# Attention splits: float16 high parts on ScalarE, remainders on GpSimd, keys and values split directly from PSUM

## The chip, the cores and the metric

The kernel runs on one core of one Trainium2 chip. The metric is the device time of one execution in microseconds. Below, PE is TensorE, DVE is VectorE, ACT is ScalarE, POOL is GpSimd and SP is SyncE, which issues every DMA of this kernel.

## The reference

One transformer-like layer over 1024 latent tokens of width 1024, with 256 context tokens as additional keys. Part of it is latent attention with 8 heads; beside it stand a Fourier mixing branch, gates, one output projection, a residual and a last norm.

```
h      = layer_norm(x) * (1 + scale) + shift            # scale, shift from silu(c)
q_lat, ckv, k_rope, gates, fourier_in = split(h @ w_in + b_in)
q      = rms_norm(q_lat) @ w_q_up                        # 8 heads of 96, rotary on 32
k, v   = rms_norm(ckv) @ w_kv_up                         # keys: context + latents = 1280
attn   = softmax(q @ k^T / sqrt(96)) @ v                 # 8 heads, 1024 queries, 1280 keys
four   = real(fft2(fourier_in)) @ w_fourier + b
y      = concat(attn * silu(g1), four * silu(g2)) @ w_out + b_out
out    = layer_norm(alpha * x + gate * y) * ln_g + ln_b
```

All inputs are float32. To be accurate enough, the kernel writes each matmul operand as a high part and a remainder ("hi" and "lo"), and adds the three leading products.

## The kernel before

Everything up to about 277 us (norms, the input projection, the queries, most of the Fourier branch) and the output projection after about 557 us keep their code. Between them lies attention.

Attention runs over 32 pairs (8 heads, 4 pairs of query tiles each). A pair has two query tiles j = 0, 1 of 128 queries against 1280 keys. For one query tile the steps are:

- `s_lat` (L135 to L137): PE writes the negated scores to the PSUM tile `SS`, three products per block of keys.
- `max_lat` (L1016) on DVE: copies `SS` to the SBUF tile `E` and keeps the row minimum; `bias` (L1023) makes the exponent's bias from it.
- `exp` (L1029) on ACT: `E` becomes the exponentials in float32, with their row sums.
- `hi` (L1040 on POOL, L1038 on ACT): the float16 high part of `E` goes to `EH`. The table `HI_CUTS` says which columns go to which engine: 0 to 639 to POOL ('p'), 640 to 1279 to ACT ('a').
- `lo` (L1046): the remainder `E - hi` in float16, also into `EH`. By `LO_CUTS`, for j = 0 DVE ('v') takes 768 columns and POOL 512; for j = 1 DVE takes 128 and POOL 1152. `HI_LAST` and `LO_LAST` are the same tables for pairs 28 to 31.
- L1050: SP issues a DMA that transposes `EH` into `ET`.
- `pv` (L1063, L1066): PE multiplies `ET` by the split V; `pv_top` (L1072, ACT) and `pv_out` (L1082, DVE) put the result away.

There are three buffers each for `E`, `EH` and `ET` (`EB`, `EHB`, `ETB`). `E` is free for a later tile when its remainder is done, `EH` when its transposing DMA has landed.

A loop over rounds n writes PE's instructions in a fixed order, given by the list `SEQ`: scores of pair n+1, `pv` of pair n-2 (`LAG`), and fills. The order of the other engines' instructions is chosen by the scheduler; each engine then works through its own queue in order. Fills are work for a later head: K^T of a pair of heads (`build_kt`, rounds 4, 5, 12, 13, 20, 21), the second group of V (`build_v(1, ...)`, rounds 14 and 15), the transposed queries (`build_qt`), from round 24 on the preparation of the output projection (`prep`, L1139, L82, L83), whose splits also go through POOL and DVE.

`build_kt` and `build_v` end in `evac`. With pool = "v" (`BP`, `BV`) ACT copies the PSUM tile to an SBUF tile `sp` (L786), POOL takes the high part from it (L787) and DVE the remainder, from `sp` and the high part (L788). With pool = False ACT writes the high part directly from PSUM (L772) and DVE reads PSUM again for the remainder (L774). `build_qt` and the first group of V already use False.

Of the kernel before, what the change touches and what calls it, by code (L numbers as in the profile page):

```python
# [21 lines left out]
P = 128  # L22
D = 1024
T = 1024
# [13 lines left out]
HI_CUTS = eval("(((0, 640, 'p'), (640, 1280, 'a')), ((0, 640, 'p'), (640, 1280, 'a')))")  # L38
LO_CUTS = eval("(((0, 768, 'v'), (768, 1280, 'p')), ((0, 128, 'v'), (128, 1280, 'p')))")
# [6 lines left out]
HI_LAST = eval("(((0, 512, 'p'), (512, 1280, 'a')), ((0, 512, 'p'), (512, 1280, 'a')))")  # L46
LO_LAST = eval("(((0, 512, 'v'), (512, 1280, 'p')), ((0, 320, 'v'), (320, 1280, 'p')))")
LATE = eval('(30, 31, 32, 33)')  # rounds at which further k-tiles of the out projection are prepared
# [6 lines left out]
BP = {"0": False, "1": True, "v": "v"}['v']  # L55
BQ = {"0": False, "1": True, "v": "v"}['0']
BV = {"0": False, "1": True, "v": "v"}['v']
BACC = {'dynamic_dma_scratch_size': int('1024')}  # no DMA is started by GpSimd
LIFT = 15.0 * math.log(2.0)  # the exponentials are scaled by 2**15 to lie well within float16
# [3 lines left out]
def tile_hybrid_block(ctx: ExitStack, tc: tile.TileContext, a, out, dbg=None):  # L63
# [6 lines left out]
    def u4(shape, dt, name):  # L70
        return big.tile(shape, dt, tag="u4", name=name)
# [35 lines left out]
    def rsqrt(y, v, n):  # L107
        """y = (v + EPS) ** -0.5 on a [P, n] tile, refined by one Newton step."""
# [22 lines left out]
    def mm3(ps, pairs, start=True):  # L131
        """ps = sum over (stationary hi, lo, moving hi, lo) of the three leading products."""
        n = len(pairs)
        for i, (sh, sl, mh, ml) in enumerate(pairs):
            nc.tensor.matmul(ps, lhsT=sh, rhs=mh, start=(start and i == 0), stop=False)  # L135
            nc.tensor.matmul(ps, lhsT=sh, rhs=ml, start=False, stop=False)  # L136
            nc.tensor.matmul(ps, lhsT=sl, rhs=mh, start=False, stop=(i == n - 1))  # L137

    # ------------------------------------------------------------ constants
# [9 lines left out]
    # partial rows of the modulation lie at partitions 32j (latents) and 32j+1 (context), two a result  # L149
# [3 lines left out]
    # PSUM pools up to the out projection, and the SBUF pool of the first phases  # L153
# [15 lines left out]
    # ------------------------------------------------------------ loads of the start  # L169
# [8 lines left out]
    class WBlock:  # L178
        """256 columns of w_in, as hi and lo parts, in two halves of k"""
# [23 lines left out]
    class WPack:  # L203
        """three blocks of 256 columns of w_in from one on, their rows in the order in which they are wanted"""
# [24 lines left out]
    mod = const.tile([P, 8, 4], F32, name="mod")  # shift_x, shift_c, 1+scale_x, 1+scale_c  # L229

    w_mod = a["w_ada"].rearrange("(k p) (s c) -> p k s c", p=P, s=3)
    GROUPS = [(i,) for i in range(8)]  # channel tiles whose modulation is worked out together
    ada, ada_ps, ada_rows = {}, {}, {}

    def load_group(g):
        """shift and scale columns of a group's channels"""
# [10 lines left out]
    def ada_mms(g):  # L247
        """partial rows of shift and scale, for the latents and for the context"""
# [11 lines left out]
    def ada_out(g):  # L260
        """their sums, transposed"""
# [44 lines left out]
    # ------------------------------------------------------------ adaLN, h^T and the Fourier input  # L306
    hT = {}  # hi and lo parts by channel tile and half of the tokens
    # the Fourier input and a first block of gates
# [5 lines left out]
    def fm_mms(ps, w, m, half, ks, parts=range(3)):  # L314
        """the leading products of the hi and lo parts, or some of them"""
# [9 lines left out]
    def x_tr(half, dt, ts=range(4)):  # L325
        """a channel tile of the normalised latents, transposed"""
# [27 lines left out]
    def h_first(half, dt):  # L354
        """the same from PSUM, without GpSimd"""
# [16 lines left out]
    def fin_out(half, g):  # L372
        """the Fourier input u as sums and differences of its token halves; the gates"""
# [15 lines left out]
    # gate of the residual branch: partial rows over halves of k, two blocks of 512 columns  # L389
# [20 lines left out]
    def gate_sums():  # L410
        """the gate itself, in the rows 0 and 64"""
# [19 lines left out]
    def warm_up(n):  # L431
        """products of no use that have TensorE's clock up when its work arrives"""
# [88 lines left out]
    # ------------------------------------------------------------ gates  # L521
# [28 lines left out]
    # ------------------------------------------------------------ token-major q | ckv | krope  # L550
# [9 lines left out]
    # tiles 0-7 hold the latents, 8 and 9 the context  # L560
# [11 lines left out]
    def rope(dst, src, cos, sin, n, eng):  # L572
        """dst[P, n, 32] = src * cos + swap_halves(src) * signed sin"""
# [28 lines left out]
    def normalise(t0, t1):  # L602
        """root-mean-square norms of q and ckv (without their weights) and the rotated key"""
# [17 lines left out]
    def latents_t(hf):  # L621
        """q and ckv of four token tiles, transposed"""
# [33 lines left out]
    ckc_k1 = u4([P, 2, 2, TC], F32R, "ckc_k1")  # and the context keys of one set  # L656
# [47 lines left out]
    with tc.manual_schedule(engines={ET.PE}):  # L704
# [11 lines left out]
        # ------------------------------------------------------------ q up-projection, token-major, with rope  # L716
# [4 lines left out]
        def tables(nm, NK):  # L721
            """hi and lo parts of a cosine and a sine table"""
# [23 lines left out]
    # ------------------------------------------------------------ Fourier mixing  # L746
# [7 lines left out]
    def ck(i, hl):  # L754
        """ckv^T of key tile i."""
# [12 lines left out]
    def evac(hi, lo, ps, pool, scale=None):  # L768
        """hi and lo parts of a PSUM tile; lo on VectorE, or from a copy on GpSimd"""
# [37 lines left out]
    def build_v(grp, i2, pool):  # L807
        if grp == 0 and i2 % 2 == 0:
            V[grp, i2 // 2] = u4([P, 2, 2, 4, 2, 64], F16, f"V{grp}{i2}")  # key tile (2), head, hi/lo, channel
# [645 lines left out]
```

## Time and profile before

| what | value |
|---|---|
| time, median of 3 runs | 655.37 us (654.37 to 655.69) |
| profiled execution: span from first to last instruction | 650.7 us |
| PE busy | 591.8 us (91%) |
| DVE busy | 467.6 us (72%) |
| ACT busy | 266.7 us (41%) |
| POOL busy | 334.6 us (51%) |
| DMA queue q1, share of 16 engines | 58.2% |
| mean granted TensorE clock | 0.956 |

The profiled execution has no time of its own beside its span; the median of the timed runs is 4.7 us above that span. Busy shares are means over stages with different limits, so a stage is read from its own stretch. Matmuls overlap in the records, so a PE that is busy all the time may still have some room.

### The profile page before, as it was taken

How to read it: one execution, taken by the hardware profiler on the slowest of the kernel's cores; microseconds unless marked ns; L12 is line 12 of the kernel's file. 1: busy time of each engine (PE TensorE's matmuls, PEld its weight loads, DVE VectorE, ACT ScalarE, POOL GpSimd, SP SyncE). 2: the span in 40 equal slices, each digit the busy share in tenths (PEclk: the TensorE clock that was granted, in tenths of full speed). 3: DMA queues.
4: the chain of work that ended last, by engine and by line, in shares of the span. 5: the costliest groups of instructions: out<-in, count | busy, mean ns of one | idle time of the engine just before them, and what ended most of it. 6: DMA issues, size and time to landing. Idle time of an engine off the chain costs nothing. (4 is left out here: it accounts for less than half of the span.)

```text
span 650.7 us, 9608 instructions
## 1 busy us (share of the span) xinstructions
PE 591.8 (91%) x3491; PEld 474.9 (73%) x3491; DVE 467.6 (72%) x806; ACT 266.7 (41%) x464; POOL 334.6 (51%) x320
## 2 busy tenths in 40 slices
PE   7999999999999999999889978897797879799995
PEld 6887777888899998987657755675475546567884
DVE  5539119501016778789789889989989989899775
ACT  2423421310124444666767765575575543100000
POOL 2023115001013294556979977897699988850000
PEclk8899999999999999999789987899798979999999
DMA  9999136000010322139989997699698998830611
GB/s 282 317 307 346 33 96 238 13 1 0 1 47 3 101 66 66 41 59 166 181 153 187 192 153 134 125 171 176 131 188 171 203 173 184 276 120 23 204 65 64
DMA packets 199703, 88.82 MB, mean 136 GB/s; under 512 B 168204, under 2 KB 189964, under 8 KB 199656
## 3 DMA queue, kind: packets, MB, share of 16 engines
q1 hardware_dynamic: 199656, 88.21, 58.2%
q8 instruction: 27, 0.44, 0.3%
q14 instruction: 20, 0.16, 0.1%
HBM read 41.39 MB, written 4.20 MB: 70 GB/s over the span
## 5 line engine op out<-in xcount | busy, mean ns | idle before, releaser
L1046 POOL TENSOR_TENSOR EH<-E,EH 128x512 f16<-128x512 f32 (+1 forms) x64 | 123.7, 1933 | 2.2 <-ACT EH L1038 0.4
L1029 ACT ACTIVATE E<-E,mx 128x1280 f32<-128x1280 f32 x64 | 87.1, 1362 | 52.3 <-DVE mx L1023 52.0
L1016 DVE TENSOR_SCALAR_CACHE_REDUCE E<-SS 128x1280 f32<-128x1280 f32 x64 | 94.9, 1484 | 12.9 <-PE SS L137 5.4
L1040 POOL TENSOR_SCALAR EH<-E 128x640 f16<-128x640 f32 (+1 forms) x64 | 63.6, 993 | 40.3 <-ACT E L1029 35.8
L1046 DVE TENSOR_TENSOR EH<-E,EH 128x768 f16<-128x768 f32 (+1 forms) x64 | 75.7, 1183 | 6.8 <-POOL EH L1040 6.3
L320 PE MATMUL fin<-h,wh 128*128 128x512 f32 x192 | 65.5, 409 | 0.0
L1063 PE MATMUL pv<-ET,V 128*128 128x256 f16 x320 | 51.3, 296 | 13.8 <-DMA ET<-EH 8.3
L320 PE MATMUL g<-h,wh 128*128 128x512 f32 x192 | 60.3, 394 | 1.0 <-DVE upm L382 1.0
L135 PE MATMUL SS<-KTh,QT 96*128 96x512 f32 x128 | 56.7, 443 | 3.6 <-DVE E L1016 3.0
L1038 ACT ACTIVATE EH<-E 128x640 f16<-128x640 f32 (+1 forms) x64 | 47.8, 747 | 14.2 <-DMA ET<-EH 13.3
L137 PE MATMUL SS<-KTh,QT 96*128 96x512 f32 x128 | 52.3, 408 | 0.0
L136 PE MATMUL SS<-KTl,QT 96*128 96x512 f32 x128 | 52.1, 407 | 0.0
L1063 PEld LDWEIGHTS <-V 128*128 128x128 f16 x320 | 28.9, 104 | 29.7 <-issue 25.3
L351 POOL TENSOR_SCALAR h<-xnT,mod 128x512 f32<-128x512 f32 x15 | 12.8, 853 | 63.6 <-DVE mod L270 30.7
L320 PEld LDWEIGHTS fin<-h,wh 128*128 128x128 f32 x192 | 36.4, 190 | 10.4 <-issue 2.9
L320 PEld LDWEIGHTS g<-h,wh 128*128 128x128 f32 x192 | 36.0, 188 | 9.8 <-issue 1.4
L320 PE MATMUL g<-h,wl 128*128 128x512 f32 x96 | 37.8, 394 | 0.0
L320 PE MATMUL fin<-h,wl 128*128 128x512 f32 x96 | 37.1, 395 | 0.0
L1066 PE MATMUL pv<-ET,V 128*64 128x256 f16 x320 | 36.6, 306 | 0.0
L135 PEld LDWEIGHTS SS<-KTh,QT 96*128 96x128 f32 x128 | 25.2, 197 | 14.1 <-issue 6.5
L1352 POOL TENSOR_TENSOR xr<-xr,lng 128x256 f32<-128x256 f32 x2 | 1.4, 722 | 66.0 <-ACT xr L1351 66.0
L111 ACT ACTIVATE rs_t<-mvf,eps 128x1 f32<-128x1 f32 x8 | 2.2, 292 | 80.5 <-DVE mvf L1342 75.2
(340 smaller groups left out, 1474.1 us busy)
## 6 DMA issues: line engine op xcount, KB each, us to landing
wada<-in_w_ada_dram SPq DMA_DIRECT2D x32, 256.0 KB, 6.4
x<-in_x_dram SPq DMA_DIRECT2D x8, 512.0 KB
wgate<-in_w_ada_dram SPq DMA_DIRECT2D x8, 512.0 KB, 6.8
wor<-in_w_out_dram SPq DMA_DIRECT2D x8, 512.0 KB, 3.9
xr<-in_x_dram SPq DMA_DIRECT2D x8, 512.0 KB, 8.5
out_dram<-xr SPq DMA_DIRECT2D x15, 256.0 KB, 2.1
wr<-in_w_in_dram SPq DMA_DIRECT2D x6, 512.0 KB, 5.5
wtr<-in_w_in_dram SPq DMA_DIRECT2D x4, 416.0 KB, 6.4
```

Of the source, the lines that this page charges most:

```text
L135: nc.tensor.matmul(ps, lhsT=sh, rhs=mh, start=(start and i == 0), stop=False)
L136: nc.tensor.matmul(ps, lhsT=sh, rhs=ml, start=False, stop=False)
L137: nc.tensor.matmul(ps, lhsT=sl, rhs=mh, start=False, stop=(i == n - 1))
L320: nc.tensor.matmul(ps, lhsT=(w.hi, w.lo, w.hi)[p][k][:, cs], rhs=h[:, p // 2], start=(k == 0 and p == 0), stop=(k == 7 and p == 2))
L351: nc.gpsimd.tensor_scalar(out=h, in0=xt, scalar1=sc, scalar2=sh, op0=ALU.mult, op1=ALU.add)
L1016: nc.vector.tensor_scalar(out=self.E[j], in0=SS[j][:, 0:1280], scalar1=0.0, scalar2=3e38, op0=ALU.add, op1=ALU.min, accum_out=self.mx[:, 2 ...
L1029: nc.scalar.activation(out=self.E[j], in_=self.E[j], func=AF.Exp, scale=-1.0, bias=self.mx[:, j:j + 1], accum_out=sums[self.h][:, qt:qt + 1])
L1038: nc.scalar.activation(out=o, in_=i, func=AF.Copy)
L1040: {"v": nc.vector, "p": nc.gpsimd}[eng].tensor_scalar(out=o, in0=i, scalar1=1.0, scalar2=0.0, op0=ALU.mult, op1=ALU.add)
L1046: {"v": nc.vector, "p": nc.gpsimd}[eng].tensor_tensor(out=self.EH[j][:, 1, cs], in0=self.E[j][:, cs], in1=self.EH[j][:, 0, cs], op=ALU.sub ...
L1063: nc.tensor.matmul(po, lhsT=v.rearrange("p l c -> p (l c)"), rhs=e, start=(kt == 0), stop=False)
L1066: nc.tensor.matmul(po[64 * g:64 * g + 64], lhsT=v[:, 0], rhs=e, start=False, stop=(kt >= 8), tile_position=(0, 64 * g))
```

## The change

The four tables of columns become one piece each: ACT writes the whole high part, POOL the whole remainder, in every pair. DVE takes no part in either any more. `BP` and `BV` become False, so that K^T of the later heads and the second group of V are split by ACT (L772) and DVE (L774) straight from PSUM. Number of buffers, PE's order of work and all sizes stay. Comments and docstrings are removed elsewhere in the file, with the lines kept in place.

```diff
-HI_CUTS = eval("(((0, 640, 'p'), (640, 1280, 'a')), ((0, 640, 'p'), (640, 1280, 'a')))")
-LO_CUTS = eval("(((0, 768, 'v'), (768, 1280, 'p')), ((0, 128, 'v'), (128, 1280, 'p')))")
+HI_CUTS = (((0, 1280, 'a'),), ((0, 1280, 'a'),))
+LO_CUTS = (((0, 1280, 'p'),), ((0, 1280, 'p'),))
...
-HI_LAST = eval("(((0, 512, 'p'), (512, 1280, 'a')), ((0, 512, 'p'), (512, 1280, 'a')))")
-LO_LAST = eval("(((0, 512, 'v'), (512, 1280, 'p')), ((0, 320, 'v'), (320, 1280, 'p')))")
+HI_LAST = HI_CUTS
+LO_LAST = LO_CUTS
...
-BP = {"0": False, "1": True, "v": "v"}['v']
+BP = False
...
-BV = {"0": False, "1": True, "v": "v"}['v']
+BV = False
```

What this moves is seen best on POOL while K^T of heads 4 and 5 is built (pairs 12 and 13). Before; `EH` rows are the splits of the exponentials, `KTh` and `ckc` high parts of K^T:

```order
L1046 TENSOR_TENSOR EH_3651<-E_3647,EH_3651 128x512
L787 TENSOR_SCALAR KTh1_2483<-sp_3690 64x512
L1040 TENSOR_SCALAR EH_3680<-E_3667 128x640
L787 TENSOR_SCALAR KTh2_2485<-sp_3694 64x512
L1046 TENSOR_TENSOR EH_3680<-E_3667,EH_3680 128x1152
L1040 TENSOR_SCALAR EH_3727<-E_3723 128x640
L787 TENSOR_SCALAR KTh1_2483<-sp_3750 64x512
L787 TENSOR_SCALAR KTh2_2485<-sp_3754 64x512
L1046 TENSOR_TENSOR EH_3727<-E_3723,EH_3727 128x512
```

The same place on POOL now:

```order
L1046 TENSOR_TENSOR EH_3591<-E_3587,EH_3591 128x1280
L1046 TENSOR_TENSOR EH_3618<-E_3605,EH_3618 128x1280
L1046 TENSOR_TENSOR EH_3657<-E_3653,EH_3657 128x1280
L1046 TENSOR_TENSOR EH_3694<-E_3673,EH_3694 128x1280
L1046 TENSOR_TENSOR EH_3733<-E_3729,EH_3733 128x1280
```

On POOL one instruction for each query tile is left where there were two, and the keys' high parts are gone from its queue.

DVE at the same place, before (`SS` to `E` is the minimum and copy, `at` the putting away of a product, `KTl` a remainder of K^T):

```order
L1016 TENSOR_SCALAR E_3723,mx_3722<-SS0_2684 128x1280
L1046 TENSOR_TENSOR EH_3651<-E_3647,EH_3651 128x768
L1023 TENSOR_SCALAR mx_3722<-mx_3722 128x1
L788 TENSOR_TENSOR KTl1_2484<-sp_3690,KTh1_2483 64x512
L1082 TENSOR_TENSOR at2_3308<-pv_3698,pvt_3719 64x256
L1046 TENSOR_TENSOR EH_3680<-E_3667,EH_3680 128x128
L1016 TENSOR_SCALAR E_3743,mx_3722<-SS1_2685 128x1280
L788 TENSOR_TENSOR KTl2_2486<-sp_3694,KTh2_2485 64x512
L1023 TENSOR_SCALAR mx_3722<-mx_3722 128x1
```

And now:

```order
L1016 TENSOR_SCALAR E_3653,mx_3652<-SS0_2684 128x1280
L774 TENSOR_TENSOR KTl1_2484<-kt20_3622,KTh1_2483 64x512
L774 TENSOR_TENSOR KTl2_2486<-kt20_3622,KTh2_2485 64x512
L1023 TENSOR_SCALAR mx_3652<-mx_3652 128x1
L1082 TENSOR_TENSOR at2_3266<-pv_3626,pvt_3649 64x256
L1016 TENSOR_SCALAR E_3673,mx_3652<-SS1_2685 128x1280
L1023 TENSOR_SCALAR mx_3652<-mx_3652 128x1
```

The remainders of the exponentials are gone from between the minimum and its bias, and those of K^T have a PSUM tile (`kt20`) as first input in place of `sp`. On ACT the order stays (exponential, high part, exponential, high part, with the copies from PSUM between); its high parts have 1280 columns in place of 640.

## Rows read from the trace of the kernel before

**Rows 1.** The page's first line.

```profile
span 650.7 us, 9608 instructions
```

**Rows 2.** Windows: stretch, length, busy us (count) of PE, PEld, DVE, ACT, POOL, clock, DMA share, GB/s.

```profile
277.56:344.93 67.37, 60.98 (x366) 47.38 (x364) 59.06 (x97) 47.05 (x75) 51.85 (x45) 0.92 0.82 145
344.93:371.63 26.70, 25.69 (x170) 19.23 (x169) 24.46 (x42) 19.18 (x30) 26.19 (x21) 1.00 1.04 186
371.63:395.11 23.48, 17.52 (x95) 12.62 (x93) 21.45 (x26) 14.09 (x24) 16.78 (x16) 0.79 0.80 140
395.11:422.43 27.32, 25.43 (x156) 18.93 (x155) 26.16 (x35) 15.85 (x26) 22.46 (x21) 0.87 0.75 141
422.43:442.24 19.81, 18.92 (x121) 14.09 (x120) 17.23 (x34) 14.87 (x24) 18.05 (x14) 1.00 0.96 177
442.24:466.55 24.31, 15.94 (x90) 11.14 (x89) 23.60 (x25) 13.15 (x23) 16.21 (x16) 0.87 0.82 149
466.55:487.65 21.10, 21.04 (x133) 15.07 (x132) 17.58 (x33) 14.67 (x22) 17.88 (x16) 0.91 0.93 177
487.65:557.49 69.84, 54.09 (x308) 37.14 (x306) 63.76 (x85) 32.75 (x49) 62.52 (x44) 0.93 0.92 182
557.49:650.70 93.21, 82.41 (x388) 66.11 (x388) 77.46 (x128) 4.71 (x12) 21.38 (x15) 0.98 0.35 124
```

**Rows 3.** Timeline, DVE, pairs 12 and 13: start, duration in us, instruction.

```profile
377.06 4.88 DVE L1046 TENSOR_TENSOR EH<-E,EH 128x128 f16<-128x128 f32 x1 [1.31 <-POOL EH L1040]
381.86 1.48 DVE L1016 TENSOR_SCALAR_CACHE_REDUCE E<-SS 128x1280 f32<-128x1280 f32 x1
...
387.40 3.54 DVE L788 TENSOR_TENSOR KTl<-sp,KTh 64x512 fp32r<-64x512 f32 x1
```

**Rows 4.** Timeline, POOL, the same stretch.

```profile
377.58 2.37 POOL L1046 TENSOR_TENSOR EH<-E,EH 128x1152 f16<-128x1152 f32 x1
379.92 0.72 POOL L1040 TENSOR_SCALAR EH<-E 128x640 f16<-128x640 f32 x1
...
381.77 1.17 POOL L1046 TENSOR_TENSOR EH<-E,EH 128x512 f16<-128x512 f32 x1
385.59 1.29 POOL L1040 TENSOR_SCALAR EH<-E 128x640 f16<-128x640 f32 x1 [2.64 <-ACT E L1029]
```

**Rows 5.** Groups by shape, attention: count, busy us, mean ns, idle before and releaser.

```profile
L1029 ACT ACTIVATE E<-E,mx 128x1280 f32<-128x1280 f32 x64 | 87.1, 1362 | 52.3 <-DVE mx L1023 52.0
L1046 POOL TENSOR_TENSOR EH<-E,EH 128x1152 f16<-128x1152 f32 x28 | 69.9, 2495 | 1.5
...
L1040 POOL TENSOR_SCALAR EH<-E 128x640 f16<-128x640 f32 x56 | 54.4, 972 | 38.1 <-ACT E L1029 33.6 <-DMA ET<-EH 4.5
...
L1038 ACT ACTIVATE EH<-E 128x640 f16<-128x640 f32 x56 | 41.1, 733 | 12.6 <-DMA ET<-EH 12.0
L1046 POOL TENSOR_TENSOR EH<-E,EH 128x512 f16<-128x512 f32 x28 | 34.6, 1236 | 0.5 <-ACT EH L1038 0.4
...
L1038 ACT ACTIVATE EH<-E 128x768 f16<-128x768 f32 x8 | 6.8, 844 | 1.5 <-DMA ET<-EH 1.3
```

**Rows 6.** Remainders of K^T on DVE, from SBUF and from PSUM: count, ns min/median/max.

```profile
L788 DVE TENSOR_TENSOR KTl<-sp,KTh x12: 672/1198/3561, 314.8 to 458.1; 64x512 fp32r<-64x512 f32 x12
...
L774 DVE TENSOR_TENSOR KTl<-kt,KTh x3: 683/692/694, 269.5 to 272.1; 64x512 fp32r<-64x512 f32 x3
```

**Rows 7.** The transposing DMAs: time of an issue on SP in ns, and us to landing.

```profile
L1050 SPq DMA_TRANSPOSE ET<-EH x64: 2990/3088/4397, 284.1 to 552.5; - x64
...
DMA to landing us min/median/max: 4.9/5.1/6.6
```

**Rows 8.** Timeline, PE: the first product with V of two rounds that follow each other.

```profile
359.17 0.70 PE L1063 MATMUL pv<-ET,V 128*128 128x256 f16 x5 [0.39 <-DVE QT L776]
...
364.99 0.72 PE L1063 MATMUL pv<-ET,V 128*128 128x256 f16 x5
```

**Rows 9.** Waits, 280 to 560 us: total us, times, longest.

```profile
ACT EH L1038 <- DMA ET<-EH: 13.3, 20, 1.4
```

## The prediction

> **What bounds the kernel now.** I first cut the span of 650.7 us [rows 1] into stretches with the table of windows, at the starts of the row minimum of a pair's first query tile (L1016), so that every stretch in attention is a whole number of rounds. From 277.56 to 487.65 there are 26 rounds, from there to 557.49 the last five and the way of the last pair to its first product [rows 2]. Three kinds of stretch are to be seen. Quiet ones (344.93 to 371.63 with four rounds, 422.43 to 442.24 with three, 466.55 to 487.65 with three) take 26.70 + 19.81 + 21.10 = 67.61 us for ten rounds, 6.76 us each. The two stretches in which K^T of a later pair of heads is built (371.63 to 395.11 and 442.24 to 466.55, two rounds each) take 23.48 + 24.31 = 47.79 us for four rounds, 11.9 us each. The one with the second group of V (395.11 to 422.43) takes 27.32 us for three, 9.1 us each. So the loss sits where fills go through POOL and DVE, and that is where I read on.
>
> In the quiet rounds four things lie close together. PE: from the first product with V of one round to the next, in a round without a fill, 364.99 - 359.17 = 5.82 us [rows 8]. SP: an issue of a transposing DMA takes 3.088 us at the median, two a round, 6.18 us [rows 7]. POOL: per round two high parts of 0.72 us, a remainder of 1.17 and one of 2.37 [rows 4], 4.98 us, and in the first quiet stretch POOL is busy 26.19 of 26.70 us [rows 2]. DVE is busy 24.46 of these 26.70.
>
> In the K^T stretches no engine but DVE is full (21.45 of 23.48 us and 23.60 of 24.31), and DVE is not working but held: its remainder of 128 columns, the smallest instruction of the kind, lasts 4.88 us from 377.06 on, and a remainder of K^T 3.54 us from 387.40 on [rows 3]; another one of that size is done in 0.672 us [rows 6]. While the first one hangs, POOL runs through its queue undisturbed: 2.37 us for 1152 columns from 377.58, the same as elsewhere, then 0.72 and 1.17 [rows 4]. So a DVE instruction with two inputs in SBUF and a POOL instruction exclude each other, and POOL, with work waiting, goes first. Behind the held instruction stands the next row minimum (it starts at 381.86, as the held one ends, rows 3), behind that the exponential on ACT, and then POOL itself has nothing to do for 2.64 us until ACT delivers [rows 4]. PE's clock falls with the stall (0.79 and 0.87 there, 1.00 in two of the quiet stretches, rows 2).
>
> **The change part by part.** *Remainders of the exponentials.* DVE's 64 instructions go. POOL's 64 get 1280 columns each. Their price from two undisturbed rows: (2.37 - 1.17) / 640 = 1.88 ns a column, so 2.37 + 128 x 0.00188 = 2.61 us; from the two means, disturbed ones among them, (2495 - 1236) / 640 = 1.97 ns, 2495 + 252 = 2747 ns [rows 4, 5]. I take 2.65 us, 5.30 us a round; the ends are 2.61 and, if every remainder cost as the longest means suggest, 2.75.
>
> *High parts.* POOL's 64 go (0.72 us undisturbed, 0.972 us at the mean of 640 columns, rows 4, 5). ACT's get 1280 columns: 733 ns for 640 and 844 ns for 768 give 0.87 ns a column, so 844 + 512 x 0.87 = 1.29 us [rows 5]. From above the exponential of the same size bounds it, 1.362 us; from below 844 ns. ACT then spends 2 x (1.36 + 1.29) = 5.30 us a round, and its copies from PSUM come on top. It has the room: it was busy 19.18 of 26.70 us in a quiet stretch [rows 2], 4.8 us a round, and gets 2 x 0.56 = 1.1 us more, 5.9 us.
>
> POOL so has 5.30 in place of 4.98 us a round, but nothing to exclude any more in most rounds: what is left on DVE reads PSUM. For one query tile the high part now precedes the whole remainder, 1.29 + 2.65 = 3.94 us, where before 0.72 + 2.37 = 3.09 followed one another on POOL for j = 1. This lengthens a pair's way to its products by about 1 us. It is hidden as long as the products come two rounds behind.
>
> *K^T and V.* 18 remainders of K^T and 5 of V change from `sp` to PSUM, and 23 POOL instructions go. From PSUM a remainder of K^T takes 0.692 us, at the median and nearly at the maximum [rows 6]; from SBUF 1.198 at the median and up to 3.561. I take 0.69 for both kinds. ACT's side is unchanged in count. The PSUM tile is held until DVE has read it twice, about 1.4 us more; PE has two such tiles, and DVE now has room.
>
> [...]
>
> *The sum, by stretches of rows 2.* The floor of a round is SP's 6.18 us; ACT's 5.9, POOL's 5.3 and PE's 5.82, each before its fills, come close to it. Four queues so near each other don't run at the floor: the ten quiet rounds stand at 6.76 us now, 0.58 above it, and I leave them there (0). The four K^T rounds lose the exclusion and keep PE's and ACT's extra work; I take 7.3 us, between the quiet 6.76 and the 7.5 us that the first stretch shows per round (67.37 for nine): 4 x 7.3 = 29.2, 18.6 us less. The three V rounds keep PE's products for V, which are real work; 8.1 us each, between 6.76 and 9.1: 24.3, 3.0 less. The first nine rounds, with two K^T rounds and the rest of the Fourier branch among them: 6.9 each, 62.1, 5.3 less. The last 69.84 us: POOL is busy 62.52 of them. Twelve high parts of about 1.1 us go there (13 us), the remainders grow by some 5.5 us; 7.5 less. There DVE's work for the output projection still excludes POOL, so no more. The last 93.21 us: PE is busy 82.41 and none of this is touched, 0. Together 18.6 + 3.0 + 5.3 + 7.5 = 34.4 us. The span would be 650.7 - 34.4 = 616.3 us. The median of the runs lies 4.7 us above the span, so 621.0 us.
>
> Bounds: if every round came to the floor of 6.18 plus 0.2 us, the quiet ones would give 4 us more, K^T 4 and the first nine 5, so about 608 us. If POOL held its remainders at 2.75 us and the last stretch gained nothing, some 10 us would be lost, 631 us.
>
> **The rivals.** *The ring of three `EH` buffers.* A high part needs a buffer whose transposing DMA has landed. High part 1.29 + remainder 2.65 + landing 5.1 [rows 7] = 9.04 us; over three buffers 3.01 us a tile, 6.03 a round, just below SP's floor. Before it was shorter by the split work. ACT already waits for it, 13.3 us in 20 waits [rows 9]. If ACT's order puts an exponential (1.36) into the ring, it is 10.4, 6.9 a round; with a landing of 6.6 us, the longest seen, 11.9, 7.9 a round. At 7.4 us the 26 rounds take 192 us in place of 210.09, and with half of the last stretch's gain it is 655.4 - 18 - 4 = 633 us.
>
> *Slower.* The same ring, in one mechanism: ACT stops in order at a high part that waits for a landing, behind it stand the next exponential and the copies from PSUM that free PE's tiles, so that PE's products and the next transposes come late, and these prolong the landing again. It decides from the point at which the mean round exceeds the present 210.09 / 26 = 8.08 us, that is a ring of 12.1 us: 3.1 us beyond the 9.04, an exponential and the longest landing and 0.2 us. At 8.4 us a round 26 rounds cost 8 us more, 663 us. Against it: transposes come 3.09 us apart at the least, so that the ring has little cause to queue for them.
>
> *POOL becomes the bound.* It would need remainders far above 2.65 us. [...] As a mechanism of this kernel, from rows: at the 2.75 us of the means 5.5 us a round, still below SP; only at 3.4 us, which no row shows, would POOL set 6.8 us and all gain beyond the stalls go. About 630 us; it is in the range of the forecast.
>
> *The change does more.* With DVE at half load the queues run closer to SP's floor: 608 us.
>
> **How the numbers follow.** Forecast (616 to 630 us) 0.50, more 0.20, the ring at about 633 to 648 us 0.18, within 0.2% of before, about what a measurement of this kernel can tell from no change, 0.03, slower by the ring 0.09. Range for 8 in 10: 603 to 644 us. Faster by over 0.2%: 0.88; same 0.03; slower 0.09.
>
> **What would show it.** Right: no DVE remainder of K^T above 0.7 us; K^T rounds of 7 to 8 us; POOL's remainders at 2.6 to 2.7 us with little spread; ACT's high parts at 1.29 us; transposes about 3.2 us apart in quiet rounds. Wrong: ACT's waits for landings growing from 13.3 us to 50 us and more (ring); POOL's remainders at 3 us or more; the stretch after the last pair's first product longer than 93 us.

## The result, and the profile after

| kernel | time, median (lowest to highest) | ratio to the kernel before, 95% interval |
|---|---|---|
| before | 655.35 us (654.37 to 655.69, 4 runs) | |
| changed | 634.82 us (632.87 to 637.83, 4 runs) | 0.9713 [0.9671, 0.9754] |

The change makes the kernel faster by 20.5 us, where 34.4 were forecast. The time lies inside the range of 603 to 644 us, 14 us above the predicted 621.0. The profiled execution is the longest of the four: 637.83 us with a span of 636.1, so that 1.7 us lie outside the span, not 4.7. With 1.7 us outside, the profiled execution of before took about 652.4 us, 2.9 below its median, while this one lies 3.0 above its own. The two profiles are therefore only 14.6 us apart (650.7 and 636.1): the stretches below show some 6 us less than the gain of the medians.

Windows of the changed kernel, cut as [rows 2] at the same row minima (the columns are those of [rows 2]):

```profile
277.23:341.65 64.42, 59.91 (x382) 45.95 (x380) 42.30 (x82) 56.10 (x75) 46.34 (x25) 0.97 0.85 153
341.65:368.88 27.23, 24.67 (x161) 18.76 (x161) 17.53 (x34) 21.93 (x30) 23.33 (x10) 1.00 1.02 183
368.88:389.03 20.15, 16.95 (x84) 12.12 (x80) 10.67 (x20) 15.92 (x23) 13.12 (x5) 0.75 1.05 185
389.03:415.52 26.49, 23.22 (x150) 17.51 (x149) 15.40 (x30) 19.23 (x27) 15.08 (x10) 0.94 0.73 131
415.52:434.85 19.33, 19.32 (x131) 14.69 (x130) 13.57 (x27) 18.03 (x23) 17.82 (x8) 1.00 0.99 180
434.85:449.54 14.69, 13.93 (x92) 10.43 (x91) 10.76 (x20) 14.53 (x22) 11.07 (x5) 1.00 1.11 190
449.54:476.27 26.73, 22.07 (x126) 15.49 (x124) 15.41 (x29) 16.42 (x22) 18.71 (x12) 0.87 0.95 175
476.27:540.70 64.43, 53.94 (x317) 37.70 (x316) 51.40 (x67) 39.38 (x50) 51.30 (x28) 0.95 1.01 193
540.70:636.10 95.40, 83.92 (x388) 66.78 (x388) 78.13 (x129) 4.71 (x12) 23.82 (x16) 0.95 0.33 121
```

DVE is relieved everywhere (10.67 in place of 21.45 us busy in the first K^T stretch), and yet that stretch falls only from 23.48 to 20.15 us at a clock of 0.75, while the second one does what was forecast (14.69). The seventh stretch is 5.6 us longer than before. That is partly the cut: a pair's row minimum comes about three rounds ahead of its first product (for pair 18 in the changed kernel at 415.52 and 435.26), and a round in which the minima fall back looks like a loss. Cut at the first product with V of pairs 11, 15, 18, 20 and 26, the kernel before reads:

```profile
379.61:421.22 41.61, 34.90 (x194) 25.60 (x194) 40.21 (x51) 23.45 (x38) 31.65 (x31) 0.79 0.70 132
421.22:442.05 20.83, 19.94 (x131) 14.66 (x129) 18.41 (x35) 14.68 (x23) 19.07 (x14) 1.00 0.92 171
442.05:466.61 24.56, 16.13 (x91) 11.32 (x91) 23.66 (x26) 13.34 (x23) 16.40 (x17) 0.87 0.82 150
466.61:511.09 44.48, 40.46 (x245) 28.68 (x244) 39.09 (x66) 28.01 (x42) 39.73 (x32) 0.92 0.92 179
```

and in the changed kernel:

```profile
378.25:415.67 37.42, 34.15 (x194) 25.24 (x195) 19.91 (x39) 26.85 (x38) 22.90 (x13) 0.83 0.81 149
415.67:435.26 19.59, 19.58 (x131) 14.68 (x129) 13.83 (x27) 18.30 (x24) 18.01 (x9) 1.00 1.00 180
435.26:451.70 16.44, 13.86 (x92) 10.38 (x91) 12.51 (x25) 16.31 (x25) 12.81 (x5) 1.00 1.10 190
451.70:495.96 44.26, 40.32 (x244) 29.32 (x245) 27.66 (x50) 31.11 (x40) 35.06 (x21) 0.92 1.01 182
```

So the second K^T stretch gives 8.1 us, and the stretch that looked like a loss is even. The first K^T stretch, with the V rounds behind it, gives 4.2 us here, but these windows begin only where PE's wait of 3.20 us (shown below) ends. The two rounds ahead of them, from the first product of pair 9 on, took 14.62 us before and 16.79 now, so that 2.0 us are left. In the three quiet rounds (415.67 to 435.26) PE is busy 19.58 of 19.59 us: it has no gap there, and `half` below tests whether it sets them.

Groups by shape of the changed kernel (count, busy us, mean ns, idle before and releasers) answer to [rows 5, 6]:

```profile
L1046 POOL TENSOR_TENSOR EH<-E,EH 128x1280 f16<-128x1280 f32 x64 | 169.3, 2650 | 51.1 <-ACT EH L1038 41.8 <-issue 5.1 <-POOL EH L1046 2.5
L1038 ACT ACTIVATE EH<-E 128x1280 f16<-128x1280 f32 x64 | 81.1, 1267 | 13.4 <-DMA ET<-EH 12.4
L774 DVE TENSOR_TENSOR KTl<-kt,KTh 64x512 fp32r<-64x512 f32 x16 | 11.0, 688 | 5.8 <-ACT KTh L772 5.5
```

The three sizes are close to those of the forecast (2.65, 1.29, 0.69 us). What was not in it is in the last column: the remainders of K^T wait 5.5 us for ACT. Timelines of ACT, DVE and PE in the first K^T stretch (start, duration, instruction, idle time before and its releaser):

```profile
372.93 1.27 ACT L1038 ACTIVATE EH<-E 128x1280 f16<-128x1280 f32 x1 [0.89 <-DMA ET<-EH]
374.11 1.35 ACT L1029 ACTIVATE E<-E,mx 128x1280 f32<-128x1280 f32 x1
...
375.57 1.20 ACT L772 ACTIVATE KTh<-kt 64x512 fp32r<-64x512 f32 x2
```

```profile
376.80 1.39 DVE L774 TENSOR_TENSOR KTl<-kt,KTh 64x512 fp32r<-64x512 f32 x2 [2.72 <-ACT KTh L772]
```

```profile
372.54 0.39 PE L137 MATMUL kt<-ckh,wk 128*128 128x512 f32 x1
...
378.25 1.25 PE L1063 MATMUL pv<-ET,V 128*128 128x256 f16 x5 [3.20 <-DVE KTl L774]
```

Read from below: PE wants a PSUM tile for `pv` and waits 3.20 us, since the tile of K^T, written at 372.9, is in DVE's hands until 378.2. DVE waited for ACT, and on ACT K^T's high parts stood behind a high part of 1280 columns, which had itself waited 0.89 us for a transposing DMA to land, and an exponential. When PE goes on, five products take 1.25 us in place of 0.72, at a granted clock of 0.50 (378 to 386 in the windows of 2 us below).

### The profile page after: what moved, and what is told of

Its sections match the earlier page's. It is cut to its first block, busy times and chain, and to the rows that moved or that the text cites. A ratio compares the mean times of both kernels' runs of the same rounds, so it can differ in the third digit from the quotient of the medians.

```text
span 636.1 us, 9339 instructions
## 1 busy us (share of the span) xinstructions
PE 587.2 (92%) x3491; PEld 472.2 (74%) x3491; DVE 391.9 (62%) x742; ACT 296.6 (47%) x464; POOL 302.1 (47%) x233
## 4 chain that ended last, share of the span: by engine, by line
PE 53%; DVE 14%; ACT 11%; DMA 8%; issue 6%; POOL 6%; SPq 1%; DVEq 0%; POOLq 0%; ACTq 0%
PE g L320 11%; PE fin L320 8%; PE SS L1154 7%; DMA ET<-EH 5%; ACT E L1029 4%; ACT EH L1038 4%; POOL EH L1046 4%; PE o L1154 3%; DVE E L1016 3%; DVE ml L83 2%; PE pv L1063 2%; PE tm L135 2%; PE tm L136 2%; PE tm L137 2%; PE SS L135 2%
## 5 line engine op out<-in xcount | busy, mean ns | idle before, releaser
L1046 POOL TENSOR_TENSOR EH<-E,EH 128x1280 f16<-128x1280 f32 x64 | 169.3, 2650 | 51.1 <-ACT EH L1038 41.8
L1038 ACT ACTIVATE EH<-E 128x1280 f16<-128x1280 f32 x64 | 81.1, 1267 | 13.4 <-DMA ET<-EH 12.4
L429 ACT ACTIVATE gt<-g,cols 128x512 f32<-128x512 f32 x12 | 8.1, 689 | 56.1 <-PE g L320 56.1
L1154 PE MATMUL SS<-woh,mh 128*128 128x512 f32 (+1 forms) x96 | 31.3, 384 | 2.4 <-POOL mh L82 1.3
```

Of the source, the lines that this page charges most:

```text
L1038: nc.scalar.activation(out=o, in_=i, func=AF.Copy)
L1046: {"v": nc.vector, "p": nc.gpsimd}[eng].tensor_tensor(out=self.EH[j][:, 1, cs], in0=self.E[j][:, cs], in1=self.EH[j][:, 0, cs], op=ALU.sub ...
L1154: nc.tensor.matmul(ps[c], lhsT=st, rhs=w[:, c[0]:c[1]], start=(i == 0 and st is mh and w is wh), stop=(i == 7 and st is ml))
```

## The experiments

**Each half of the change alone.** `e1_tables` keeps the tables of the changed kernel, `e2_keys` the PSUM splits:

```diff
 e1_tables (from the changed kernel)     e2_keys (from the kernel before)
-BP = False                              -BP = {"0": False, "1": True, "v": "v"}['v']
+BP = "v"                                +BP = False
-BV = False                              -BV = {"0": False, "1": True, "v": "v"}['v']
+BV = "v"                                +BV = False
```

> The changed kernel with only its float16 tables (high part of a tile wholly on ScalarE, remainder wholly on GpSimd); K^T and the second V go by the copy, GpSimd's high part and VectorE's remainder, as before. Theory (the two halves of the change need each other: a VectorE remainder that reads two SBUF operands loses its turn beside GpSimd's 2.65-us remainders, and the K^T tiles add GpSimd high parts to a GpSimd that now holds the whole remainder): the two K^T stretches stay at 20 us or more each (23.5 and 24.3 before, 20.2 and 14.7 with the whole change), the first nine rounds and the last stretch gain as they did (64.4 and 64.4), total 643 to 652 us. Rival (the tables do all): 633 to 638 us, K^T stretches 20 and 15 us. Rival (the tables alone do harm): above 655 us.

> The kernel before with K^T and the second V split from PSUM by ScalarE and VectorE, the float16 tables as before. Theory: VectorE is relieved of nothing (its remainder from PSUM takes about the 0.69 us of that from SBUF) but the step over GpSimd goes; the K^T stretches fall from 23.5 and 24.3 to 17 to 20 us each, the other stretches stay, total 642 to 650 us. Rival (the PSUM splits are the whole gain): 633 to 638 us. Rival (nothing without the tables): 653 to 657 us.

Measured: `e1_tables` 645.2 us (0.9868 [0.9839, 0.9897]), `e2_keys` 643.8 us (0.9838 [0.9792, 0.9884]). The two gains, 1.3% and 1.6%, add up to the 2.9% of the whole: the halves work side by side and don't need each other, against what I had written for `e1_tables`. Both times lie in the ranges of their theories, the stretches only in part. By the row minima, the two K^T stretches take 22.87 and 18.69 us in `e1_tables` (20 or more expected) and 18.50 and 21.21 in `e2_keys` (17 to 20), and the first nine rounds of `e1_tables` did not gain (69.05 us). What held is that a VectorE remainder with two SBUF inputs loses its turn, to be seen in `e1_tables` at its plainest. DVE's two K^T remainders from SBUF, and POOL beside them:

```profile
381.40 6.80 DVE L788 TENSOR_TENSOR KTl<-sp,KTh 64x512 fp32r<-64x512 f32 x2
```

```profile
381.10 2.64 POOL L1046 TENSOR_TENSOR EH<-E,EH 128x1280 f16<-128x1280 f32 x1
383.72 0.40 POOL L787 TENSOR_SCALAR KTc<-sp 64x256 fp32r<-64x256 f32 x1
384.09 0.40 POOL L787 TENSOR_SCALAR ckc_k<-sp 64x256 fp32r<-64x256 f32 x1
384.46 2.60 POOL L1046 TENSOR_TENSOR EH<-E,EH 128x1280 f16<-128x1280 f32 x1
```

Two instructions that take 0.67 us undisturbed [rows 6] take 6.80 together. POOL goes through its queue without a gap until 387.06, its instructions take no longer than elsewhere, and DVE is done 1.1 us after that. From PSUM, in the changed kernel, the same two take 1.39 us although POOL is at work all that time:

```profile
369.33 2.64 POOL L1046 TENSOR_TENSOR EH<-E,EH 128x1280 f16<-128x1280 f32 x1 [0.49 <-ACT EH L1038]
```

```profile
370.46 1.39 DVE L774 TENSOR_TENSOR KTl<-kt,KTh 64x512 fp32r<-64x512 f32 x2
```

The exclusion that the prediction read from [rows 3, 4] is confirmed.

**The load of w_out's tile 4, earlier.** In the changed kernel DVE waits 3.8 us for that load from 459 on, ahead of a row minimum's bias. `FT` names the rounds in which fills stand, 'g' the one from which the gate's rows are loaded, which go ahead of this load.

```diff
-FT = eval("{..., 'g': 22, 's': [24, 27]}")
+FT = eval("{..., 'g': 18, 's': [24, 27]}")
```

> The changed kernel with one number altered: the gate's rows are loaded from round 18 on, not 22, which lets the scheduler put out the load of w_out's tile 4 four rounds earlier. Theory (the round of 14.58 us at 449.5 to 464.1 is VectorE queued behind that load: DVE 3.8, POOL 5.8 and ACT 8.8 us of waits in a chain): that round falls to 7 to 8 us and the whole to 627 to 630 us. Rival (the round is late for another reason, K^T's copies or the queue of SP): the load is early but the round stays above 12 us and the total at 633 to 637 us.

Measured 632.1 us (0.967 [0.9627, 0.9714], overlapping the changed kernel's interval). The load is issued only 7.4 us earlier (449.6 in place of 457.0), DVE still waits 4.1 us for it, and the round by row minima takes 13.4 us. The edit did not take the wait away, so it decides nothing on its cost; by the cut at the products, the rounds from pair 18 to pair 26 take 60.55 us in place of 60.70.

It showed something else. Up to that place it runs as the changed kernel does, round for round, and PE's wait in the first K^T stretch is the same, 3.10 us. But the round behind it took 9.99 us (378.46 to 388.45) in place of 12.94 (378.25 to 391.19). Windows of 2 us there, in the changed kernel (the clock is the third number from the end):

```profile
376.00:378.00 2.00, 0.00 (x0) 0.00 (x0) 1.18 (x2) 1.99 (x4) 0.95 (x1) 0.87 0.78 147
378.00:380.00 2.00, 1.75 (x10) 0.94 (x10) 1.84 (x4) 1.96 (x5) 1.94 (x1) 0.50 1.01 193
...
384.00:386.00 2.00, 2.00 (x9) 1.56 (x8) 0.14 (x1) 0.01 (x1) 1.86 (x1) 0.50 0.97 185
386.00:388.00 2.00, 2.00 (x8) 1.65 (x7) 1.74 (x4) 0.76 (x2) 0.75 (x1) 0.57 1.13 217
```

and with the early load:

```profile
378.00:380.00 2.00, 1.54 (x9) 0.91 (x10) 1.93 (x4) 1.97 (x5) 1.73 (x1) 0.50 0.89 171
380.00:382.00 2.00, 2.00 (x16) 0.89 (x12) 0.96 (x3) 2.00 (x3) 1.32 (x2) 0.65 0.84 161
382.00:384.00 2.00, 2.00 (x12) 1.66 (x12) 0.00 (x0) 2.00 (x4) 2.00 (x1) 1.00 1.04 200
```

After the same wait the granted clock stays at 0.50 for some 9 us in one execution and 3 us in the other. PE's busy time differs by as much as the rounds do (11.10 and 8.18 us). Behind the next wait, of 1.84 and 1.81 us, the clock is low again in the changed kernel (0.50 from 392 to 394) and full with the early load, and that round takes 9.40 and 7.94 us, PE busy throughout. So 4.4 us of difference in these two rounds are the clock alone, behind waits of the same length; why it differs, no run shows. The spread of the changed kernel's own runs, 5 us, may well be this; single profiles are compared here with that in mind.

**K^T's splits at once.** The changed kernel collects the splits of a fill and puts them out at the next place that `SEQ` has for them. `late0` puts each out where its product is:

```diff
-                        late["on"] = n > 0
+                        late["on"] = False
```

> The changed kernel with the splits of K^T, V and Q^T issued where their products are, not gathered to the next gathering point of the order. Theory (the first K^T stretch takes 20.2 us, not the 14.6 forecast, since K^T's high parts stand behind a whole tile's high part and exponential on ScalarE and the PSUM tile is held until VectorE has done both remainders): first K^T stretch 15 to 17 us, the second 14 to 16; the load of w_out's tile 4 comes earlier too, so that round 23 falls below 10 us; total 624 to 631 us. Rival (the splits' place has no part in it): K^T stretches stay at 20 and 15 us, only the round of the load changes, 627 to 632 us. Rival (issued early, they delay the row minima and ScalarE's exponentials): K^T and V stretches longer by 2 us each, total 636 to 645 us.

Measured 652.5 us (0.9962 [0.994, 0.9985]): 17.7 us slower than the changed kernel, more than any of the three said. Nearest is the third: the scheduler put the row minimum between the two remainders of a K^T tile. DVE's timeline:

```profile
371.87 0.68 DVE L774 TENSOR_TENSOR KTl<-kt,KTh 64x512 fp32r<-64x512 f32 x1
...
376.42 0.69 DVE L774 TENSOR_TENSOR KTl<-kt,KTh 64x512 fp32r<-64x512 f32 x1 [0.93 <-ACT KTh L772]
378.38 0.68 DVE L774 TENSOR_TENSOR KTl<-kt,KTh 64x512 fp32r<-64x512 f32 x1 [1.21 <-ACT KTh L772]
...
381.77 0.69 DVE L774 TENSOR_TENSOR KTl<-kt,KTh 64x512 fp32r<-64x512 f32 x1 [0.20 <-ACT KTh L772]
```

In a round that began 1.6 us later than in the changed kernel (370.45 and 368.88), the first tile is held until 377.1 in place of 371.8, the second until 382.5 in place of 378.2, and `pv` waits 4.73 us there. Over attention (290 to 545 us) PE's waits of `pv` for `KTl` grow from 5.9 to 11.0 us, each three times. Held longer, the tile costs more. But 8 us of the 17.7 lie in the last stretch, after the last pair's first product (103.4 in place of 95.4 us), and what they come from was not looked into.

**K^T spread over three rounds.**

```diff
-FT = eval("{'k': [0, 0, 1], ...}")
+FT = eval("{'k': [0, 1, 2], ...}")
```

> The changed kernel with one number altered: the three products that build a pair of heads' K^T stand in rounds 0, 1 and 2 of a head and no longer in 0, 0 and 1, so that no two of them hold both PSUM tiles at once. Theory (a K^T round loses because the tiles of two K^T products are held until VectorE has subtracted twice from each, the product with V waits for one of them, 5.9 us in three waits, and TensorE comes back at the lower clock, 0.63 and 0.77 in such rounds): the waits for KTl fall below 2 us, the mean clock goes up to 0.97 or more, total 624 to 631 us. Rival (the wait moves to the tile of Q^T or of V that comes next): waits of the same sum behind another name, total 633 to 639 us.

> The same, and the gate's rows loaded from round 18 on. Theory: the two add up, 2 to 3 us below the kernel with K^T spread alone, 621 to 629 us, clearly below the changed kernel. Rival (they cost the same time, that of a late round 23): no faster than either alone, 630 to 634 us.

Measured 639.4 us (0.9767 [0.9746, 0.9787]), and with the early load 633.9 us (0.9681 [0.9658, 0.9705]). The wait of `pv` for `KTl` is gone, and the kernel isn't faster for it. With the early load its time lies in the rival's range, no better than that of the early load alone (632.1 us). PE's longest waits in attention with K^T spread (us in total, times, longest):

```profile
PE pv L1063 <- DMA ET<-EH: 13.5, 9, 3.5
PE SS L135 <- DVE E L1016: 6.8, 6, 3.0
PE qh L827 <- DVE at L1082: 3.8, 1, 3.8
```

The wait moved, as the rival had it, though not to Q^T's tile foremost: `pv` now waits for its own transposes, 13.5 us in place of 6.5. That asked for the next pair.

**What sets a round: transposes or products.** `half` transposes the high parts alone (its products with the remainders read the blocks of the high parts), `nolo` leaves out ten products in each round:

```diff
 half
-            nc.sync.dma_start(out=self.ET[:, j], in_=self.EH[j].rearrange("p l k -> p (l k)"), transpose=True)
+            nc.sync.dma_start(out=self.ET[:, j, 0:10], in_=self.EH[j][:, 0], transpose=True)
...
 nolo
-            for hl in range(2):
+            for hl in range(1):
...
```

> The changed kernel in which only the high parts are transposed, 10 blocks of 128 columns a DMA in place of 20; the products with the remainders read the high parts' blocks, so that the transposing of the remainders is left out of the computation and every other instruction stays. It asks what sets a quiet round. Theory (TensorE: in the three quiet rounds of the changed kernel, from the first product with V of pair 15 to that of pair 18, it was busy 19.58 of 19.59 us): these three rounds stay at 19.3 to 19.7 us, total 629 to 636 us. Rival (SP, which takes 3.1 us for an issue and 6.18 us a round, the floor of my sum): an issue gets shorter and the three rounds fall to 17 to 18.5 us, total 612 to 624 us.

> The changed kernel without TensorE's ten products of V with the remainders in each round (left out of the computation); transposes and all work of the other engines stay. Theory (TensorE sets the quiet rounds, and SP's 6.18 us a round lies close behind): ten products at 0.104 us apart are 1.04 us a round, but the three quiet rounds fall only from 19.59 to 18.5 to 18.9 us, total 615 to 626 us. Rival (SP or POOL sets the round already): the three rounds stay above 19.3 us, total 631 to 636 us. Rival (nothing stands close behind TensorE): 16.5 us, total 600 to 608 us.

Measured: `half` 618.3 us (0.9454 [0.9432, 0.9476]), `nolo` 627.3 us (0.9592 [0.957, 0.9615]). Windows of `half` that answer to the four of the cut at the products:

```profile
368.29:399.99 31.70, 28.45 (x194) 22.16 (x195) 19.92 (x39) 26.56 (x38) 22.93 (x13) 1.00 0.44 84
399.99:419.58 19.59, 19.58 (x131) 14.68 (x129) 13.83 (x27) 18.29 (x24) 18.03 (x9) 1.00 0.58 102
419.58:436.02 16.44, 13.86 (x92) 10.38 (x91) 12.50 (x25) 16.31 (x25) 12.79 (x5) 1.00 0.64 102
436.02:475.27 39.25, 37.00 (x245) 27.71 (x245) 28.23 (x45) 30.36 (x39) 34.04 (x21) 1.00 0.65 125
```

Theory and rival of `half` hold one part each. The quiet rounds stay at 19.59 us with half the transposing, so transposes do not set them. The total is in the rival's range: the first K^T stretch with the V rounds gets 5.7 us shorter and the stretch from pair 20 on 5.0, with the clock at 1.00 in both. The second K^T stretch, which had the full clock already, stays at 16.44 us. Ahead of the first K^T window `pv` waits 1.22 us for `KTl` in place of 3.20, and ACT no longer waits for a landing ahead of it. `nolo` is the other side: PE has 32 x 1.04 = 33 us of products less (an estimate: five of the ten take 0.52 us in the changed kernel's trace), the kernel gains 7.5, its time lies in none of the three ranges, and `pv` waits for transposes instead:

```profile
PE pv L1063 <- DMA ET<-EH: 21.3, 14, 4.4
```

Its three quiet rounds took 22.4 us, not 18.5 to 18.9: the rounds ahead of them had run faster (26.5 us in place of 37.4 from pair 11 to 15), and `pv` waits 3.5 us for transposes in them.

**SP's time, or the way over GpSimd.** `half` takes two things away: the transpose gets smaller (SP's issue falls from 3.11 to 1.34 us, the landing from 5.1 to 3.4), and it doesn't wait for the remainder. `half2` takes away only the second, `halflo` only the first; both leave out part of the computation:

```diff
 half2
+            for l in range(2):
+                nc.sync.dma_start(out=self.ET[:, j, 10 * l:10 * l + 10], in_=self.EH[j][:, 0], transpose=True)
...
 halflo
+            nc.sync.dma_start(out=self.ET[:, j, 0:10], in_=self.EH[j][:, 1], transpose=True)
...
```

> The changed kernel in which each tile's high part is transposed twice, in two DMAs of 10 blocks, into the place of the high parts and into that of the remainders; the transposing of the remainders is left out of the computation, so no transpose waits for GpSimd. SP's time is kept: an issue of 10 blocks took 1.34 us, two are 2.67, against 3.11 for the one of 20. It tells apart what the kernel with half the transposes gained by (618.3 us). Theory (the way from the exponential to the products, on which GpSimd's 2.65 us now stands alone for each tile): 618 to 624 us. Rival (SP's time, 6.2 us a round in a round of 7.9): 629 to 636 us.

> The changed kernel in which only the remainders are transposed, in one DMA of 10 blocks, and the products with the high parts read the remainders' blocks (the transposing of the high parts is left out of the computation). The transpose waits for GpSimd as in the changed kernel, SP's issue is 1.34 us in place of 3.11 and the landing 3.4 us after its start in place of 5.1. Theory (the way over GpSimd): only the 1.7 us of the earlier landing is gained, 627 to 633 us. Rival (SP's time): 617 to 622 us, as with the high parts alone.

Measured: `half2` 639.4 us (0.9784 [0.975, 0.9817]), `halflo` 617.4 us (0.9451 [0.9423, 0.948]). My theory falls: `halflo` is in the rival's range, and `half2` lies above every range, 3.4 us beyond the rival's. The 26 rounds from the first product of pair 0 to that of pair 26 take 199.31 us in the changed kernel and 180.22 in `half`. Of these 19.1 us, 11.3 are PE's own busy time (180.70 and 169.37 us for the same products), at a mean clock of 0.94 and 1.00. In `halflo`:

```profile
295.30:475.51 180.21, 170.74 (x1119) 128.61 (x1116) 125.11 (x230) 161.52 (x216) 150.44 (x75) 0.99 0.56 103
```

With short transposes the 2.65 us on GpSimd cost nothing at all (180.22 and 180.21 us). With SP's time kept (two issues of 1.53 us), `half2` needs

```profile
294.82:486.83 192.01, 177.17 (x1119) 132.12 (x1117) 132.05 (x237) 164.21 (x219) 152.79 (x75) 0.95 1.04 187
```

so some 7 of the 19 us come with that too. They need not come from GpSimd: in `split2` below, where the transpose is cut in two as well but the remainders still go over GpSimd, these rounds take 194.94 us, and 190.21 with the early load. As a whole `half2` is slower for a thing of its own: after the last pair, from 525.07 on, it takes 112.43 us in place of 95.40, with one wait of PE in it,

```profile
PE SS L1155 <- POOL mh L82: 15.5, 1, 15.5
```

where the scheduler put DVE's work on the residual ahead of w_out's last tiles. So the amount that is transposed counts for the other 12. Whether it is the issue on SP or the DMA engines' work was not separated, as both shrink together (DMA share 1.04 and 0.56 in the two rows). The earlier landing, and with it the ring of `EH` buffers, can account for the 7 us of `half2` at most: ACT's waits for it fall from 12.4 us to 0.9 in `half2` already, and to 0.2 in `halflo`.

**The transposes cut in two, complete kernels.**

```diff
+            nc.sync.dma_start(out=self.ET[:, j, 0:10], in_=self.EH[j][:, 0], transpose=True)
             for c0, c1, eng in (LO_LAST if self.n >= NLAST else LO_CUTS)[j]:
...
+            nc.sync.dma_start(out=self.ET[:, j, 10:20], in_=self.EH[j][:, 1], transpose=True)
...
```

> The changed kernel, complete, with each tile's transposing DMA cut in two: that of the high part is issued as soon as ScalarE has written it, that of the remainder after GpSimd. Theory (GpSimd's remainder on the way to the products): the first ten products of a round, with the high parts, no longer wait for it, and SP's time falls from 6.2 to 5.4 us a round; 622 to 630 us. Rival (the second DMA of a tile lands as late as the one before did and the products with the remainders wait for it in the same place): 631 to 637 us. Rival (SP, in order, waits in front of a remainder's DMA and holds the next tile's high part behind it, and twice as many issues queue): 637 to 650 us.

> The same, and the gate's rows loaded from round 18 on, which alone gave 632.1 us against 634.8. Theory: 2 to 3 us below the kernel with the cut transposes alone, 619 to 628 us, faster than every complete kernel so far. Rival: the early load changes nothing where the transposes have room, the same time as without it within 1 us.

Measured 642.7 us (0.9846 [0.9819, 0.9872]) and 642.6 us (0.9852 [0.9809, 0.9896]). Both are slower than the theories said. `split2` lies in the range of its last rival, but not by that mechanism, and the early load adds nothing, as its rival said. The 26 rounds gain (194.94 and 190.21 us in place of 199.31), and the stretch after the last pair's first product, longer here as in `half2`, takes it back (113.0 and 112.3 us). Two issues of 10 blocks took 1.47 us each at the median, 2.94 together, hardly less than the one of 3.11. No complete kernel was clearly faster than the changed one; with the last stretch in the changed kernel's order this one might be, which was not tried.

## Why the forecast was right in sign and too large

- **The mechanism was right.** Exclusion of DVE by POOL is what the change removes: no K^T remainder above 0.694 us, POOL's remainders at 2.65, and, in `e1_tables`, two K^T remainders from SBUF stretched to 6.80 us. That the second K^T stretch came out at 14.69 us, against 4 x 7.3 / 2 = 14.6, is partly luck of the cut: at the products it takes 16.44, and the stretch behind it at the row minima is 5.6 us longer than before.
- **The four K^T rounds: 18.6 us forecast, 3.3 + 9.6 = 13.0 measured** by the cut of [rows 2]. The step that failed is "the PSUM tile is held about 1.4 us more; PE has two such tiles, and DVE now has room". DVE had room, ACT had not: its queue stood in front of the high parts. The tile was held for 5.3 us, PE waited 3.2 and came back at a clock of 0.50, so that the wait was paid twice. How much the second payment is varies: in the profile of `g18`, which has the same wait, the K^T and the V stretch take 17.09 and 25.02 us by the same cut, where the profile of the changed kernel, its slowest execution, has 20.15 and 26.49. So 4.5 us of what is missing here come and go from one execution to another. In `late0` the wait grows with the hold; `k012` shows that removing that wait alone brings nothing, since `pv` then waits for transposes.
- **"The floor of a round is SP's 6.18 us"** was the step behind it. It is not the floor of a quiet round: PE with its fills is, at 6.53 us (19.59 / 3), where I had taken 5.82 without them. But the terms for the disturbed rounds (7.3, 8.1, 6.9 us) held no time for the transposes to catch up after a stall, with 2 x 3.11 = 6.22 us of issues in a round of 6.53. `half` and `halflo` show the price: with transposes of half the size the whole comes to 617 or 618 us, below the forecast. Of the 19.1 us that `half` gives in the 26 rounds, 6.3 lie up to pair 9, 2.1 from there to pair 11, 5.7 to pair 15, none in the second K^T stretch and 5.0 from pair 20 on. That it is SP's queue rather than the DMA engines' work is argued, not shown. The three V rounds gave 0.8 us, not 3.0, the first nine 3.0, not 5.3.
- **The last stretches.** By the cut of [rows 2] 5.4 of 7.5 us came, but the stretch ahead, which was to stay, lost 5.6; at the products, from pair 26 to the last pair, it is 46.40 - 44.74 = 1.7 us. The final stretch grew by 2.2 us at a clock of 0.95 against 0.98, where 0 was forecast and more than 93 us was named as a sign of being wrong. It takes 93.96 us in `g18` and 92.73 in `halflo`; I have no experiment on it.
- **The quiet rounds** stayed, as forecast, in two of the three stretches: 27.23 and 19.33 against 26.70 and 19.81. The third is the one with 26.73 in place of 21.10, which is even at the products.
- **4.7 us outside the span** was wrong: it is about 1.7 in the executions on record, so the profiled execution of before was simply shorter than its median. With 1.7 the same sum gives 618.0 us.
- **The rivals.** The ring of `EH` buffers: ACT waits 12.4 us for landings, 13.3 before [rows 9], so it is not what took the gain as I had priced it; but one of these waits, 0.89 us, heads the chain above, and with halved transposes they vanish. GpSimd as the bound: no, `halflo` has it fully on the way at no cost (180.21 us for the 26 rounds, 180.22 in `half`), though only with short transposes. The trace shows its remainders slower than VectorE's: 2.65 us for 1280 columns are 2.07 ns a column, against 1.34 ns for VectorE's 512 columns from PSUM in 0.688 us. The tables as a whole paid all the same (1.3% in `e1_tables`), since GpSimd had time, 302 us busy of 636.

## What to carry to other kernels

An engine or queue that lies just below the round's floor need not be free: here the size of the transposes cost nothing in three quiet rounds (19.59 us with all of them and with half) and 5.7 us from pair 11 to 15, behind the stall, so compare it with the disturbed rounds too, and test it by halving its work. When a copy in PSUM is replaced by two readers, count what stands in front of the first reader on its engine (here, for K^T, a high part of 1.27 us that had waited 0.89, and an exponential of 1.35), and add the time at the lower clock to PE's wait (3 to 9 us at 0.50 after 3.1 to 3.2 us). Before you compare stretches, set each profiled execution against the median of its kernel, since one execution can differ from the next by several microseconds in a single stretch (4.4 us in two rounds between the changed kernel and `g18`). Cut stretches at the engine that sets the pace; cut elsewhere, a round in which a forerunner falls back looks like a loss.

## What the hardware showed that was not expected

- After the same idle time of 3.1 to 3.2 us PE ran at a granted clock of 0.50 for some 3 us in one execution (`g18`) and 9 us in another (the changed kernel). After 1.8 us in the same two it came back at 1.00 in the first and at 0.50 in the second; after 1.22 us, in `half`, five products took 0.72 us, and the clock of that stretch was 1.00.
- A transposing DMA of 10 blocks had an issue of 1.34 us and landed 3.4 us after its start (`half`); one of 20 blocks 3.11 and 5.1 us (the changed kernel). Two of 10 close together took 1.53 us each (`half2`).
- A DVE subtraction of 64x512 with both inputs in SBUF was stretched from 0.67 to 3.4 us, two of them 6.80 us, beside back-to-back POOL work (`e1_tables`); with one input in PSUM all 16 stayed between 0.677 and 0.694 us (the changed kernel).
